# All SBUF tiles begin at one place in a line of 256 bytes, and the small vectors get a pool of their own

## The chip, the core and the metric

The kernel runs on one core of a Trainium2 chip. The core has a matrix engine (TensorE, PE in the profile; its weight loads are listed as PEld), a vector engine (VectorE, DVE), an activation engine (ScalarE, ACT), GpSimd (POOL) and SyncE (SP), whose queue issues nearly all DMAs. Data lies in SBUF, 128 partitions wide; a tile takes the same byte range in every partition. Matmul results go to PSUM. The metric is the device time of one execution in microseconds, as the median of several runs.

## What is computed

One layer of a diffusion backbone over 1024 latent tokens and 256 context tokens, width 1024, all in fp32. In a much shortened form:

```
h       = rms_norm(x) * (1 + m1) + m0                  # m = silu(c) @ w_mod + b_mod
aq, ak, av, bq, bk, bv, cq, cf, cb, ci, cg, gates = split(h @ w_in)
ya      = window_attn(aq, ak, av, context, sink)       # 8 heads, window 128, keys of the context, sink
yb      = global_attn(bq, bk, bv, context)             # 8 heads, 256 + 1024 keys
yc      = hgrn2_bidir(cq, cf, cb, ci, cg, ...)         # 4 heads, recurrence in both directions
x_mix   = x + m2 * ((sum over n of sigmoid(gates_n) * (y_n @ w_branch_n)) @ w_out)
h2      = rms_norm(x_mix) * (1 + m4) + m3
a, g    = split(dwconv(h2 @ w_up))                     # depthwise, 3 taps
out     = rms_norm(x_mix + m5 * ((a * silu(g)) @ w_down))
```

## The kernel before

Every large product is done in three passes: each fp32 operand is split into a high part (a cast to fp32r, on ScalarE) and a low part (the difference, a subtraction on VectorE), and the products high x high, high x low and low x high are summed in PSUM. In `gemm_cm` these are lines L160 (`wh`, `hh`), L161 (`wh`, `hl`) and L162 (`wl`, `hh`), in this order for each of the 128-row blocks of the contraction. The weights are the stationary operand, the activations are the moving one, 512 columns at a time. In `gemm_tm` (L170 to L172) it is the other way round: the moving operand is the weights, 256 columns.

`w_unit` brings a unit of weights: a DMA on SP's queue into `wr` (L142), the cast to `wh` on ScalarE (L145), the difference `wl` on VectorE (L146), three buffers each. The units are requested some steps ahead of the product that reads them.

The stages, with the tiles that stream through TensorE as the moving operand:

- context and latent norm, context projections (`czf`, `czb`, `czv`: moving `chh`, `chl`, 256 columns)
- HGRN2, four heads: projections `zq`, `zf`, `zb`, `zv`, `zg` (moving `hh`, `hl`, 512 columns) and many small matmuls
- token-major projections `tm`, with the products for the gates, `gz` (moving `hh`, `hl`), in between
- window attention and then global attention, 16 iterations each (8 token tiles x 2 groups). Scores of the next iteration, values of the present one and more `gz` products are woven into each other. `values` transposes probabilities (`pp`, L983), splits them (`ph` on ScalarE, L987; `pl` on VectorE, L988) and streams `ph` and `pl` against the values (`po`, L977 and L978). The global scores stream the keys (`sbl`, L1097 and L1098)
- merge (`br`: moving `yh`, `yl`)
- output projection `wo` in two halves of 512 tokens (moving `h2h`, `h2l`, which hold the merged branches there); VectorE adds the residual `xr` (L601), which a DMA on SP's queue brings (L600)
- FFN: `up` (moving `h2h`, `h2l`, now the normed activations) and `dn` (moving `ah`, `al`), in seven groups; the last group (`dl`) and the final norm run in three pieces of 512, 256 and 256 tokens

`softmax_window` and `softmax_global` keep their statistics in small tiles with two buffers each: negated maxima (`wm`, `ng`), sums (`ws`, `sm`), the sink's term (`wk`), factors (`fa`, `mn`). The first instruction that writes a buffer again waits for the last reader of two iterations before; the last one is the scaling of the probabilities on GpSimd (L1070, L1117 and L1119).

The tiles come from pools that lie on two stacks, one from the low end of SBUF, one from the high end (`side="right"`). A tile's place follows from the sizes of what was allocated before it, rounded to 32 bytes. Small tiles (16 bytes, 32 bytes) between large ones shift all that come after them within a line of 256 bytes.

The order in which each engine takes its instructions is fixed when the program is built; priorities (`tc.high_priority`) move the weights' steps ahead.

Of the kernel before, what the change touches and what calls it, by code (L numbers as in the profile page):

```python
# [9 lines left out]
F32 = mybir.dt.float32  # L10
F32R = mybir.dt.float32r
U32 = mybir.dt.uint32
AF = mybir.ActivationFunctionType
# [5 lines left out]
P = 128  # L19
D = 1024  # L20
KT = D // P
# [45 lines left out]
U_C = {"q": 0, "f": 4, "b": 8, "v": 12, "g": 16, "gate": 20}  # L67


class Ctx:  # L70
    pass


def build(tc, ins, out, dbg=None):
    nc = tc.nc
    V, A, G, T, SP = nc.vector, nc.scalar, nc.gpsimd, nc.tensor, nc.sync
    with ExitStack() as top:
        const = top.enter_context(tc.tile_pool(name="const", bufs=1))
        wp = top.enter_context(tc.tile_pool(name="wp", bufs=3))
        ps = top.enter_context(tc.tile_pool(name="ps", bufs=2, space=PSUM))  # L80
        dp = top.enter_context(tc.tile_pool(name="dp", bufs=1, space=DRAM))

        def ct(shape, name, dt=F32):
            return const.tile(shape, dt, tag=name, name=name)

        def dt_(shape, name, dt=F32):
            return dp.tile(shape, dt, tag=name, name=name)
# [5 lines left out]
            return ps.tile(list(shape), dt, tag=tag, name=name)  # L93


        ones = ct([P, P], "ones")
        V.memset(ones, 1.0)
        mhalf = ct([P, 8], "mhalf")
        V.memset(mhalf, -0.5)
        cc = ct([P, KT, 2], "cc")  # L100
        SP.dma_start(cc, ins["cc"])

        tmpv = ct([P, KT, 2], "tmpv")
        A.activation(tmpv, ones[:, :KT * 2].rearrange("p (k v) -> p k v", v=2), AF.Sigmoid)
        A.activation(tmpv, cc, AF.Sigmoid)
        scc = ct([P, KT, 2], "scc")
        V.tensor_tensor(out=scc, in0=cc, in1=tmpv, op=ALU.mult)
        gains = ct([P, 3, KT], "gains")
        SP.dma_start(gains, ins["gains"])
        bmod = ct([P, 48], "bmod")  # L110
        SP.dma_start(bmod, ins["b_mod"])
        ident = ct([P, P], "ident")
        SP.dma_start(ident, ins["ident"])
        lbr = ct([P, 8], "lbr")
        gnc = ct([P, 1], "gnc")
        identr = ct([P, P], "identr", F32R)
        G.tensor_copy(identr, ident)
        mods = ct([P, 4, KT], "mods")
        af = ct([P, KT], "a_ffn")
        m01 = ct([P, KT, 2, 2], "m01")  # L120
        a01 = ct([P, KT, 2], "a01")
        lb = ct([P, 8], "lbt")
        oml = ct([P, 8], "oml")


        q_d = [dt_([LT, P, 512], f"q_d{b}") for b in range(2)]
# [89 lines left out]
            V.scalar_tensor_tensor(out=ohl, in0=t, scalar=bi, in1=ohh.bitcast(F32), op0=ALU.add, op1=ALU.subtract)  # L216

        with ExitStack() as s0:
            xp = s0.enter_context(tc.tile_pool(name="xp", bufs=1, side="right", reuse_waits="tile"))
# [3 lines left out]
            xq = xin.enter_context(tc.tile_pool(name="xq", bufs=1, side="right", reuse_waits="tile"))  # L223
# [3 lines left out]
            xm_ = xw.enter_context(tc.tile_pool(name="xm_", bufs=1))  # L227

            hc = (chh, chl)
            units0 = []  # L230
# [30 lines left out]
            for i in range(KT):  # L261
                wm = xm_.tile([P, 2, KT, P], F32, tag="wm", name=f"wm{i}", bufs=WM)
# [39 lines left out]
            SP.dma_start(lbr, ins["lb"])  # L302
            SP.dma_start(gnc, ins["gn"])

            lt = ct([P, 8], "lt")
# [9 lines left out]
            hp = hpool.enter_context(tc.tile_pool(name="hp", bufs=1, reuse_waits="tile"))  # L315
# [3 lines left out]
            sp_ = stx.enter_context(tc.tile_pool(name="sp_", bufs=1, reuse_waits="tile"))  # L319
# [28 lines left out]
            cp = s0.enter_context(tc.tile_pool(name="cp", bufs=1, reuse_waits="tile"))  # L348
# [52 lines left out]

            weave((ctx_all(), 14), (lat_norm(), 13))
            xin.close()
            cp2 = s0.enter_context(tc.tile_pool(name="cp2", bufs=1, reuse_waits="tile"))

            Fp = cF
            B = 1
# [73 lines left out]


        with ExitStack() as sc:
            c1 = sc.enter_context(tc.tile_pool(name="c1", bufs=1, side="right", reuse_waits="tile"))
# [10 lines left out]


        with ExitStack() as sp3:
            p3 = sp3.enter_context(tc.tile_pool(name="p3", bufs=2, side="right", reuse_waits="tile"))
# [55 lines left out]
        n0 = 10 + GATES_A  # L554
        for br, units in ((0, gates[10:n0]), (1, gates[n0:])):
            with ExitStack() as sa:
                ap_ = sa.enter_context(tc.tile_pool(name=f"at{br}", bufs=2, side="right", reuse_waits="tile"))
# [8 lines left out]
        fp = top.enter_context(tc.tile_pool(name="fp", bufs=1, side="right", reuse_waits="tile"))  # L566
        xm = fp.tile([P, KT, L], F32, tag="xm", name="xm")
        f2 = top.enter_context(tc.tile_pool(name="f2", bufs=1, side="right", reuse_waits="tile"))
        h2h = f2.tile([P, KT, L], F32R, tag="h2h", name="h2h")
        h2l = f2.tile([P, KT, L], F32R, tag="h2l", name="h2l")  # L570
        with ExitStack() as sm:
            mp = sm.enter_context(tc.tile_pool(name="mp", bufs=2, reuse_waits="tile"))
            merge_up(nc, mp, ins, gate_d, y_d, xm, h2h, h2l, w_unit, gemm_cm, mm2)
        f3 = ExitStack()
        ff = f3.enter_context(tc.tile_pool(name="ff", bufs=2, reuse_waits="tile"))
        cw = ff.tile([P, 2 * FT, 4], F32, tag="cw", name="cw", bufs=1)
        SP.dma_start(cw, ins["conv"])

# [13 lines left out]
        for hf in range(2):  # L592
            cols = slice(hf * 512, hf * 512 + 512)
            ss = []
            for i in range(KT):
                w = w_unit(ins["w_out"][i], KT, P)
                z = bank("b", f"wo{hf}{i}", (P, 512))
                gemm_cm(z, w, (h2h, h2l), cols)
                xr = ff.tile([P, 512], F32, tag="o", name=f"xr{hf}{i}", bufs=3)
                SP.dma_start(xr, ins["xT"][i * P:(i + 1) * P, cols])  # L600
                V.scalar_tensor_tensor(out=xm[:, i, cols], in0=z, scalar=mods[:, 0, i:i + 1], in1=xr,  # L601
                                       op0=ALU.mult, op1=ALU.add)
# [43 lines left out]
        for g, ng in enumerate(FFN_GROUPS):  # L646
# [15 lines left out]
            else:  # L662
# [21 lines left out]
                for bi, n in enumerate(LAST):  # L684
# [349 lines left out]
def softmax_window(nc, tl, mm2, tt, g, nm, QT, KH, KL, trir, identr, snk, nsnk, res):  # L1034
    V, A, G, T = nc.vector, nc.scalar, nc.gpsimd, nc.tensor
# [3 lines left out]
    w = nk - 256  # L1039
    m0 = (lo - (tt - 1)) * P  # L1040
    Ps = []
    ng = tl([P, 4], "wm", nm)
    sm = tl([P, 4], "ws", nm)
    sk = tl([P, 4], "wk", nm)
    for h in range(4):

        sc = mm2(f"sa{nm}{h}").rearrange("p a b -> p (a b)")[:, 256:256 + nk]
        T.matmul(sc[:, :256], QT[:, h], KH[:, g, :256], start=True, stop=False)
        T.matmul(sc[:, :256], QT[:, h], KL[:, g, :256], start=False, stop=True)
        k = (2 + lo) * P  # L1050
# [192 lines left out]
```

## Time and profile before

| | us |
|---|---|
| median of 3 runs | 2242.84 |
| lowest and highest run | 2238.89, 2244.82 |
| profiled execution, its own time | 2242.07 |
| span of the profiled execution | 2240.3 |

The granted clock of TensorE over the span is 0.992 of full speed. A profile is one execution. Each row of a group says line, engine, operation, tiles out<-in (moving operand first for a matmul, then the stationary one), shape, count, then busy us and the mean ns of one, then the idle time of the engine just before them and what ended it. Rows of windows say from:to in us of the span, then busy us and the number of records per engine. Rows of the timeline say start, duration, engine, line, operation. A DMA is listed at its issue on SP's queue and by its time to landing.

### The profile page before, as it was taken

Reading aid. Unit: us, or ns where it says so; the run is one execution under the profiler, and the core shown is the slowest. Engines: PE = TensorE matmul, PEld = TensorE weight load, DVE = VectorE, ACT = ScalarE, POOL = GpSimd, SP = SyncE. Lnnn points to the kernel's source line nnn. Section 1 sums busy time; section 2 is a strip of 40 time slices with the busy share of each in tenths; the row PEclk is TensorE's granted clock in tenths of the full one; section 3 lists DMA queues with packets and bytes.
Section 4 is the critical chain, followed back from the end, with each engine's and each line's share of the span. In section 5 each row is a group of like instructions: output and inputs, shape, how many; then the busy total and the mean of one; then the engine's idle time right before and its main releaser. Section 6 shows DMA issues by size and latency. Waiting matters only on the chain. (4 is left out here: it accounts for less than half of the span.)

```text
span 2240.3 us, 30805 instructions
## 1 busy us (share of the span) xinstructions
PE 2158.9 (96%) x11912; PEld 1778.5 (79%) x11912; DVE 1358.5 (61%) x2426; ACT 888.6 (40%) x1618; POOL 285.4 (13%) x297
## 2 busy tenths in 40 slices
PE   7799999999999999999999999999999999999997
PEld 4778887888988888777777788778888888888876
DVE  6946656636665777599998657554434344444345
ACT  4523323311123777677777534332222122222223
POOL 1410011010021222133323100100000000000004
PEclk9999999999999999999999999999999999999999
DMA  8320111126543211301100554421110202111112
GB/s 312 118 65 29 48 48 34 53 93 214 186 150 126 60 46 53 97 21 31 34 29 27 179 178 142 132 85 34 43 61 24 70 21 69 33 56 56 33 52 76
DMA packets 80242, 180.14 MB, mean 80 GB/s; under 512 B 9056, under 2 KB 38240, under 8 KB 79072
## 3 DMA queue, kind: packets, MB, share of 16 engines
q1 hardware_dynamic: 79808, 178.11, 24.5%
q8 instruction: 94, 1.54, 0.3%
q14 instruction: 52, 0.43, 0.1%
q10 hardware_dynamic: 288, 0.07, 0.0%
HBM read 148.26 MB, written 29.88 MB: 80 GB/s over the span
## 5 line engine op out<-in xcount | busy, mean ns | idle before, releaser
L145 ACT CAST wh<-wr 128x1024 fp32r<-128x1024 f32 (+2 forms) x194 | 179.6, 927 | 737.7 <-PE up L161 301.8
L146 DVE TENSOR_TENSOR wl<-wr,wh 128x1024 fp32r<-128x1024 f32 (+2 forms) x189 | 206.8, 1094 | 380.8 <-ACT wh L145 379.0
L161 PE MATMUL up<-h2l,wh 128*128 128x512 f32 x704 | 279.1, 397 | 0.0
L160 PE MATMUL up<-h2h,wh 128*128 128x512 f32 x704 | 278.4, 396 | 0.0
L162 PE MATMUL up<-h2h,wl 128*128 128x512 f32 x704 | 276.5, 393 | 0.0
L988 DVE TENSOR_TENSOR pl<-pp,ph 128x512 fp32r<-128x512 f32 x236 | 158.8, 683 | 9.7 <-ACT ph L987 8.2
L160 PEld LDWEIGHTS up<-h2h,wh 128*128 128x128 f32 x704 | 132.1, 188 | 32.9
L160 PE MATMUL gz<-hh,wh 128*128 128x512 f32 x384 | 155.4, 405 | 2.9 <-ACT gs L450 2.8
L162 PEld LDWEIGHTS up<-h2h,wl 128*128 128x128 f32 x704 | 132.2, 188 | 32.3
L161 PEld LDWEIGHTS up<-h2l,wh 128*128 128x128 f32 x704 | 132.2, 188 | 31.0 <-DVE h2l L216 0.3
L987 ACT CAST ph<-pp 128x512 fp32r<-128x512 f32 x236 | 136.3, 585 | 43.1 <-PE pp L983 40.4
L162 PE MATMUL gz<-hh,wl 128*128 128x512 f32 x384 | 151.5, 395 | 0.0
L161 PE MATMUL gz<-hl,wh 128*128 128x512 f32 x384 | 151.4, 394 | 0.0
L160 PE MATMUL dn<-ah,wh 128*128 128x512 f32 x320 | 125.8, 393 | 0.4
L161 PE MATMUL dn<-al,wh 128*128 128x512 f32 x320 | 125.7, 393 | 0.0
L162 PE MATMUL dn<-ah,wl 128*128 128x512 f32 x320 | 124.7, 390 | 0.0
L660 DVE SCALAR_TENSOR_TENSOR xm<-dn,mods,xm 128x1024 f32<-128x1024 f32 x48 | 61.6, 1283 | 88.7 <-PE dn L162 88.2
L171 PE MATMUL tm<-wl,hh 128*128 128x256 f32 x384 | 108.9, 283 | 2.6 <-DVE wl L146 2.6
L170 PE MATMUL tm<-wh,hh 128*128 128x256 f32 x384 | 108.7, 283 | 0.0
L172 PE MATMUL tm<-wh,hl 128*128 128x256 f32 x384 | 108.6, 283 | 0.0
L977 PE MATMUL po<-ph,VHL 128*128 128x512 f32 x236 | 105.4, 447 | 1.3 <-ACT ph L987 1.3
L978 PE MATMUL po<-pl,VHL 128*128 128x512 f32 x236 | 99.2, 420 | 7.6 <-DVE pl L988 7.3
(825 smaller groups left out, 5045.0 us busy)
## 6 DMA issues: line engine op xcount, KB each, us to landing
wr<-in_w_cm SPq DMA_DIRECT2D x56, 512.0 KB, 3.8
wr<-in_w_up SPq DMA_DIRECT2D x44, 512.0 KB, 3.6
wmr<-in_w_mod SPq DMA_DIRECT2D x32, 512.0 KB, 4.6
gate_d<-gs SPq DMA_DIRECT2D x48, 256.0 KB, 2.3
sgt<-gate_d SPq DMA_DIRECT2D x24, 512.0 KB, 3.8
wm<-in_w_mod SPq DMA_DIRECT2D x8, 1024.0 KB, 14.2
wr<-in_w_tm SPq DMA_DIRECT2D x16, 512.0 KB, 3.8
wr<-in_w_out SPq DMA_DIRECT2D x16, 512.0 KB, 3.8
```

Of the source, the lines that this page charges most:

```text
L145: A.copy(hi[:, :n], raw[:, :n])
L146: (lo_eng or V).tensor_tensor(out=lo[:, :n], in0=raw[:, :n], in1=hi[:, :n].bitcast(F32), op=ALU.subtract)
L160: T.matmul(psl, wh[:, k, c], hh[:, k0 + k, cols], start=s, stop=False)
L161: T.matmul(psl, wh[:, k, c], hl[:, k0 + k, cols], start=False, stop=False)
L162: T.matmul(psl, wl[:, k, c], hh[:, k0 + k, cols], start=False, stop=e)
L170: T.matmul(psl, hh[:, k, toks], wh[:, k % 4, :], start=s, stop=False)
L171: T.matmul(psl, hh[:, k, toks], wl[:, k % 4, :], start=False, stop=False)
L172: T.matmul(psl, hl[:, k, toks], wh[:, k % 4, :], start=False, stop=e)
L977: T.matmul(po, vv, ph, start=n == 0, stop=False)
L978: T.matmul(po, vv, pl, start=False, stop=n == len(kts) - 1)
L987: A.copy(ph, pp)
L988: V.tensor_tensor(out=pl, in0=pp, in1=ph.bitcast(F32), op=ALU.subtract)
```

## The change

1. A class `Aligned` wraps every SBUF pool. It rounds a tile's free size up to a multiple of 64 fp32 numbers, 256 bytes, and returns a view of the part that was asked for.
2. The vectors of a few numbers (`ones`, `mhalf`, `cc`, `scc`, `gains`, `bmod`, `mods`, `lbr` and others) go to a pool `small`, which isn't wrapped; a tile `rest` fills it up. `ones` shrinks from 128 columns to the 16 that are read. `lb`, `oml` and `lt` become slices of one tile.
3. A tile `edge` of 96 bytes at the top of the right stack brings that stack to the same place in the line as the left one.
4. `xr` has two buffers and not three.
5. The statistics of the softmaxes become slices of one tile `st` (two buffers).

Where tiles begin, in bytes within a line of 256, by the addresses of the two built programs:

| tiles | before | after |
|---|---|---|
| wr, wh, wl; wm; hh, hl; cK, cF, cV; yh, yl, y, sgt | 128 | 128 |
| chh, chl | 224 | 128 |
| cx, x32, their squares | 192 | 128 |
| HGRN2: qr, KS, QQ, Vt, S, KC; ST, kt, yo, ys | 224; 160 | 128 |
| tables and outputs of the token-major stage; wmr | 160 | 128 |
| KH, KL, VHL; pw, plat, pc, ph, pl, yT | 224 | 128 |
| QT, qf, qs (window; global) | 32; 224 | 128 |
| xm, h2h, h2l | 224 | 128 |
| xr, squares of the output projection | 64 | 128 |
| u, sg, ah, al, ht | 192 | 128 |

The low-end stack as a whole moves down by one line of 256 bytes: hh began at 220 x 256 + 128, now at 219 x 256 + 128; hl, wr, wh, wl, yh and yl likewise. h2h and h2l keep their line (511 and 639) and move within it.

```diff
+class Aligned:
+    def __init__(self, pool):
+        self.pool = pool
+    def tile(self, shape, dt, **kw):
+        n = math.prod(shape[1:])
+        m = -(-n // 64) * 64
+        if m == n:
+            return self.pool.tile(shape, dt, **kw)
+        t = self.pool.tile([shape[0], m], dt, **kw)[:, :n]
...
-        const = top.enter_context(tc.tile_pool(name="const", bufs=1))
-        wp = top.enter_context(tc.tile_pool(name="wp", bufs=3))
+        const = Aligned(top.enter_context(tc.tile_pool(name="const", bufs=1)))
+        small = top.enter_context(tc.tile_pool(name="small", bufs=1))
+        small.tile([P, 48], F32, tag="rest", name="rest")
+        wp = Aligned(top.enter_context(tc.tile_pool(name="wp", bufs=3)))
...
+        edge = top.enter_context(tc.tile_pool(name="edge", bufs=1, side="right"))
+        edge.tile([P, 24], F32, tag="edge", name="edge")
...
-        f2 = top.enter_context(tc.tile_pool(name="f2", bufs=1, side="right", reuse_waits="tile"))
+        f2 = Aligned(top.enter_context(tc.tile_pool(name="f2", bufs=1, side="right", reuse_waits="tile")))
...
-                xr = ff.tile([P, 512], F32, tag="o", name=f"xr{hf}{i}", bufs=3)
+                xr = ff.tile([P, 512], F32, tag="o", name=f"xr{hf}{i}", bufs=2)
...
-    ng = tl([P, 4], "wm", nm)
-    sm = tl([P, 4], "ws", nm)
-    sk = tl([P, 4], "wk", nm)
+    st = tl([P, 8, 4], "st", nm)
+    ng, sm, sk = st[:, 0], st[:, 1], st[:, 2]
...
-    ng = tl([P, 2, 4], "ng", nm)
-    sm = tl([P, 2, 4], "sm", nm)
-    mn = tl([P, 4], "mn", nm)
-    fa = tl([P, 2, 4], "fa", nm)
+    st = tl([P, 8, 4], "st", nm)
+    ng, sm, fa, mn = st[:, 0:2], st[:, 2:4], st[:, 4:6], st[:, 6]
```

Every engine's instructions keep their order, with one exception on SP's queue in the output projection. `xr02` is the residual block of the third output tile of the first half, `wr91` the weights of the seventh; what an instruction waits for stands in brackets. Before:

```order
L600 DMA xr01_13976<-in_xT 128x512 [waits DMAHW3_49,PE_49]
L600 DMA xr02_14013<-in_xT 128x512 [waits DMAHW4_49]
L600 DMA xr03_14050<-in_xT 128x512 [waits DMAHW5_49,DMAHW2_49,DVE_49]
L142 DMA wr91_14129<-in_w_out 128x1024 [waits DMAHW6_49,DVE_49]
L600 DMA xr04_14087<-in_xT 128x512 [waits DMAHW7_49,DMAHW3_49,DVE_49]
L142 DMA wr92_14166<-in_w_out 128x1024 [waits DMAHW0_49,DVE_49]
```

And now:

```order
L623 DMA xr01_13902<-in_xT 128x512 [waits DMAHW3_49,PE_49]
L623 DMA xr02_13939<-in_xT 128x512 [waits DMAHW4_49,DMAHW2_49,DVE_49]
L166 DMA wr91_14055<-in_w_out 128x1024 [waits DMAHW5_49,DVE_49]
L623 DMA xr03_13976<-in_xT 128x512 [waits DMAHW6_49,DMAHW3_49,DVE_49]
L166 DMA wr92_14092<-in_w_out 128x1024 [waits DMAHW7_49,DVE_49]
```

The residual's DMA that waits for the first product on VectorE is now the third and not the fourth, and each later one stands one place further back relative to the weights; the weights keep their order and their own wait on VectorE.

On VectorE the order stays, and one wait moves. The third iteration of the window attention (`sa` are its scores), before:

```order
L1056 TENSOR_REDUCE wm_2__6768<-sa_0_6771 128x1 [waits PE_49]
L988 TENSOR_TENSOR pl_10_6793<-pp_6787,ph_10_6792 128x512 [waits Activation_49]
L1058 TENSOR_TENSOR wm_2__6768<-wm_2__6768,nsnk_0_6284 128x1 [waits DVE_49]
L1056 TENSOR_REDUCE wm_2__6768<-sa_1_6799 128x1 [waits PE_49]
L1065 TENSOR_TENSOR wk_2__6770<-snk_0_6282,wm_2__6768 128x1 [waits DVE_49]
L953 SCALAR_TENSOR_TENSOR qs_q_7063<-qf_q_7061,qs_q_7063 128x4x64 [waits DMAHW3_49]
L1067 TENSOR_TENSOR ws_2__6769<-ws_2__6769,wk_2__6770 128x1 [waits Activation_49,Pool_49]
```

And now:

```order
L1078 TENSOR_REDUCE st_2__6770<-sa_0_6771 128x1 [waits PE_49,Pool_49]
L1011 TENSOR_TENSOR pl_10_6793<-pp_6787,ph_10_6792 128x512 [waits Activation_49]
L1080 TENSOR_TENSOR st_2__6770<-st_2__6770,nsnk_0_6290 128x1 [waits DVE_49]
L1078 TENSOR_REDUCE st_2__6770<-sa_1_6799 128x1 [waits PE_49]
L1087 TENSOR_TENSOR st_2__6770<-snk_0_6288,st_2__6770 128x1 [waits DVE_49]
L976 SCALAR_TENSOR_TENSOR qs_q_7061<-qf_q_7059,qs_q_7061 128x4x64 [waits DMAHW3_49]
L1089 TENSOR_TENSOR st_2__6770<-st_2__6770 128x1 [waits Activation_49]
```

The wait for GpSimd (`Pool`) moved from the first sum to the first maximum, six instructions ahead; it is for the same GpSimd instruction, the last scaling of two iterations before. In the global attention the like wait moved from the exponentials on ScalarE to the maximum on VectorE ahead of them.

More of the change, by code (lines that the diff above doesn't have):

```diff
@@ L67 @@
 U_C = {"q": 0, "f": 4, "b": 8, "v": 12, "g": 16, "gate": 20}
-class Ctx:
-    pass
+class Aligned:
[7 more added lines that the diff above has]
+        t = self.pool.tile([shape[0], m], dt, **kw)[:, :n]
+        if len(shape) == 2:
+            return t
+        d = "abc"[:len(shape) - 1]
+        return t.rearrange(f"p ({' '.join(d)}) -> p {' '.join(d)}", **dict(zip(d, shape[1:])))
 def build(tc, ins, out, dbg=None):
@@ L77, in build, with cs @@
     with ExitStack() as top:
[L78 to L79 removed]
+        const = Aligned(top.enter_context(tc.tile_pool(name="const", bufs=1)))
+        small = top.enter_context(tc.tile_pool(name="small", bufs=1))
+        small.tile([P, 48], F32, tag="rest", name="rest")
+        wp = Aligned(top.enter_context(tc.tile_pool(name="wp", bufs=3)))
         ps = top.enter_context(tc.tile_pool(name="ps", bufs=2, space=PSUM))
         dp = top.enter_context(tc.tile_pool(name="dp", bufs=1, space=DRAM))
+        edge = top.enter_context(tc.tile_pool(name="edge", bufs=1, side="right"))
+        edge.tile([P, 24], F32, tag="edge", name="edge")
         def ct(shape, name, dt=F32):
             return const.tile(shape, dt, tag=name, name=name)
+        def cs(shape, name, dt=F32):
+            return small.tile(shape, dt, tag=name, name=name)
         def dt_(shape, name, dt=F32):
@@ L113, in build @@
         SP.dma_start(ident, ins["ident"])
-        lbr = ct([P, 8], "lbr")
-        gnc = ct([P, 1], "gnc")
+        lbr = cs([P, 8], "lbr")
+        gnc = cs([P, 1], "gnc")
         identr = ct([P, P], "identr", F32R)
         G.tensor_copy(identr, ident)
[L118 to L123, printed above, removed]
+        mods = cs([P, 4, KT], "mods")
+        af = cs([P, KT], "a_ffn")
+        m01 = cs([P, KT, 2, 2], "m01")
+        a01 = cs([P, KT, 2], "a01")
+        lbs = cs([P, 3, 8], "lbs")
+        lb, oml, lt = lbs[:, 0], lbs[:, 1], lbs[:, 2]
         q_d = [dt_([LT, P, 512], f"q_d{b}") for b in range(2)]
@@ L218, in build @@
         with ExitStack() as s0:
-            xp = s0.enter_context(tc.tile_pool(name="xp", bufs=1, side="right", reuse_waits="tile"))
+            xp = Aligned(s0.enter_context(tc.tile_pool(name="xp", bufs=1, side="right", reuse_waits="tile")))
             chh = xp.tile([P, KT, LC], F32R, tag="chh", name="chh")
@@ L222, in build @@
             xin = s0.enter_context(ExitStack())
-            xq = xin.enter_context(tc.tile_pool(name="xq", bufs=1, side="right", reuse_waits="tile"))
+            xq = Aligned(xin.enter_context(tc.tile_pool(name="xq", bufs=1, side="right", reuse_waits="tile")))
             cx = xq.tile([P, KT, LC], F32, tag="cx", name="cx")
@@ L314, in build @@
             hpool = top.enter_context(ExitStack())
-            hp = hpool.enter_context(tc.tile_pool(name="hp", bufs=1, reuse_waits="tile"))
+            hp = Aligned(hpool.enter_context(tc.tile_pool(name="hp", bufs=1, reuse_waits="tile")))
             hh = hp.tile([P, KT, L], F32R, tag="hh", name="hh")
@@ L403, in build @@
             xin.close()
-            cp2 = s0.enter_context(tc.tile_pool(name="cp2", bufs=1, reuse_waits="tile"))
+            cp2 = Aligned(s0.enter_context(tc.tile_pool(name="cp2", bufs=1, reuse_waits="tile")))
             Fp = cF
@@ L483, in build @@
         with ExitStack() as sc:
-            c1 = sc.enter_context(tc.tile_pool(name="c1", bufs=1, side="right", reuse_waits="tile"))
+            c1 = Aligned(sc.enter_context(tc.tile_pool(name="c1", bufs=1, side="right", reuse_waits="tile")))
             masks = c1.tile([P, NMASK, HB], U32, tag="masks", name="masks")
@@ L497, in build @@
         with ExitStack() as sp3:
-            p3 = sp3.enter_context(tc.tile_pool(name="p3", bufs=2, side="right", reuse_waits="tile"))
+            p3 = Aligned(sp3.enter_context(tc.tile_pool(name="p3", bufs=2, side="right", reuse_waits="tile")))
             cs = p3.tile([P, LT, 2, 32], F32, tag="cs", name="cs", bufs=1)
@@ L556, in build @@
             with ExitStack() as sa:
-                ap_ = sa.enter_context(tc.tile_pool(name=f"at{br}", bufs=2, side="right", reuse_waits="tile"))
+                ap_ = Aligned(sa.enter_context(tc.tile_pool(name=f"at{br}", bufs=2, side="right", reuse_waits="tile")))
                 nf = 16 * len(units)
@@ L563, in build @@
         hpool.close()
-        fp = top.enter_context(tc.tile_pool(name="fp", bufs=1, side="right", reuse_waits="tile"))
+        fp = Aligned(top.enter_context(tc.tile_pool(name="fp", bufs=1, side="right", reuse_waits="tile")))
         xm = fp.tile([P, KT, L], F32, tag="xm", name="xm")
-        f2 = top.enter_context(tc.tile_pool(name="f2", bufs=1, side="right", reuse_waits="tile"))
+        f2 = Aligned(top.enter_context(tc.tile_pool(name="f2", bufs=1, side="right", reuse_waits="tile")))
         h2h = f2.tile([P, KT, L], F32R, tag="h2h", name="h2h")
```

27 lines of the change are left out of this document (13 added, 14 removed).

## The prediction

> **What bounds the kernel now.** I read the page's first two parts, then the busy time by stage, then the start times of single matmuls.
>
> ```profile
> span 2240.3 us, 30805 instructions
> PE 2158.9 (96%) x11912; PEld 1778.5 (79%) x11912; DVE 1358.5 (61%) x2426; ACT 888.6 (40%) x1618; POOL 285.4 (13%) x297
> PE   7799999999999999999999999999999999999997
> ```
>
> TensorE is busy from the second slice to the last but one. Busy time by stage (window and its length, then busy us and number of records for PE, PEld, DVE, ACT, POOL; the granted clock, the DMA share and GB/s):
>
> ```profile
> 723.00:936.00 213.00, 210.38 (x1240) 178.65 (x1239) 155.99 (x469) 152.90 (x385) 49.52 (x64) 1.00 0.21 65
> 936.00:1246.00 310.00, 289.94 (x1621) 231.26 (x1620) 280.02 (x667) 232.37 (x552) 102.07 (x128) 1.00 0.11 35
> 1246.00:1386.60 140.60, 139.08 (x619) 112.92 (x618) 85.47 (x79) 59.77 (x64) 0.00 (x0) 1.00 0.54 174
> 1386.60:1480.00 93.40, 92.57 (x405) 73.82 (x405) 50.15 (x62) 32.47 (x41) 10.59 (x7) 1.00 0.42 136
> 1480.00:2180.00 700.00, 699.15 (x3016) 564.06 (x3015) 304.56 (x283) 168.27 (x184) 1.02 (x1) 1.00 0.15 46
> ```
>
> The rows are window attention, global attention, merge, output projection and FFN. In the FFN the PE works 699 of 700 us at full clock, VectorE 305, ScalarE 168, the DMAs 15%. So there the time is matmuls times the distance from one start to the next, and nothing else comes near. In the global attention VectorE (280 of 310) is nearly as full as the PE (290).
>
> A matmul's record (390 ns) overlaps its neighbour's, so I take starts, not durations. First and last L160 of four stretches in the order of time, and the number of records in the same stretches:
>
> ```profile
> 159.03 0.39 PE L160 MATMUL zv<-hh,wh 128*128 128x512 f32 x1
> ...
> 169.24 0.39 PE L160 MATMUL zv<-hh,wh 128*128 128x512 f32 x1
> ...
> 1400.04 0.40 PE L160 MATMUL wo<-h2h,wh 128*128 128x512 f32 x1
> ...
> 1420.34 0.40 PE L160 MATMUL wo<-h2h,wh 128*128 128x512 f32 x1
> ...
> 1600.10 0.39 PE L160 MATMUL dn<-ah,wh 128*128 128x512 f32 x1
> ...
> 1620.01 0.39 PE L160 MATMUL dn<-ah,wh 128*128 128x512 f32 x1
> ...
> 1700.15 0.39 PE L160 MATMUL up<-h2h,wh 128*128 128x512 f32 x1
> ...
> 1719.75 0.39 PE L160 MATMUL up<-h2h,wh 128*128 128x512 f32 x1
> ```
>
> ```profile
> 158.80:169.67 10.87, 10.87 (x49) 1.00 0.14 49
> 1400.04:1421.03 20.99, 20.99 (x91) 1.00 0.46 152
> 1600.10:1620.68 20.58, 20.58 (x91) 1.00 0.22 64
> 1700.15:1721.14 20.99, 20.99 (x91) 1.00 0.10 25
> ```
>
> The lines follow each other in threes (L160, L161, L162), so the pairs lie 45, 87, 87 and 84 matmuls apart. Start to start: zv 10.21/45 = 226.9 ns, wo 20.30/87 = 233.3, dn 19.91/87 = 228.9, up 19.60/84 = 233.3. (Each count holds one record that began before the window.) Four streams of the same shape, with the same kind of weights, no waits and clock 1.00, run at three speeds. What goes along with the speed is where the moving operand begins in a 256-byte line (table of the section on the change): hh at 128, ah and al at 192, h2h and h2l at 224. The weights begin at 128 in all four.
>
> **The change, part by part.** Groups that carry the sum (busy us, mean ns of one record, idle before):
>
> ```profile
> L160 PE MATMUL up<-h2h,wh 128*128 128x512 f32 x704 | 278.4, 396 | 0.0
> L160 PE MATMUL gz<-hh,wh 128*128 128x512 f32 x384 | 155.4, 405 | 2.9 <-ACT gs L450 2.8
> L160 PE MATMUL dn<-ah,wh 128*128 128x512 f32 x320 | 125.8, 393 | 0.4
> L160 PE MATMUL br<-yh,wh 128*128 128x512 f32 x192 | 74.4, 390 | 1.1 <-DVE xm L1156 1.1
> L160 PE MATMUL wo<-h2h,wh 128*128 128x512 f32 x128 | 51.1, 401 | 0.3 <-ACT h2h L1161 0.3
> L160 PE MATMUL zv<-hh,wh 128*128 128x512 f32 x64 | 24.9, 389 | 0.0
> L977 PE MATMUL po<-ph,VHL 128*128 128x512 f32 x236 | 105.4, 447 | 1.3 <-ACT ph L987 1.3
> L1097 PE MATMUL sbl<-KH,QT 128*128 128x512 f32 x128 | 51.8, 404 | 0.0
> ```
>
> *New starts.* The three lines of each projection have the same count, L977/L978 and L1097/L1098 too. After the change every moving operand begins at 128, as hh does now, so I give all of them zv's 226.9 ns.
> - up: 3 x 704 = 2112 matmuls x (233.3 - 226.9 = 6.4 ns) = 13.5 us.
> - wo: 3 x 128 = 384 x 6.4 = 2.5 us.
> - dn: 3 x 320 = 960 x 2.0 = 1.9 us; the 512-column part of the last group (dl, 8 tiles x 6 = 48 matmuls, as the code has it) 0.1 us.
>
> These 18.0 us lie on the path in full, since the PE there waits for nothing. Their other end: yh, also at 128, has a mean record of 390 ns against zv's 389; 1 ns on 3504 matmuls is 3.5 us less.
> - Attention: 256 sbl and 472 po move from 224 to 128: at most 728 x 6.4 = 4.7 us. VectorE is nearly as busy there and the PE has gaps, so the gain lies between 0 and 4.7; I take the middle, 2.3.
> - gz streams hh, which begins at 128 before and after: nothing. But its mean record (405) is above zv's (389) where it stands among other matmuls; its three lines average some 9 ns over zv, 1152 x 9 = 10 us with waits in it. If half comes from neighbours at 224, another 5 us go. I take 0 and keep 5 for the low end.
>
> Shorter matmuls I count at nothing: 256 columns that begin at 128 (tm) and at 224 (czv) have the same mean record:
>
> ```profile
> L171 PE MATMUL tm<-wl,hh 128*128 128x256 f32 x384 | 108.9, 283 | 2.6 <-DVE wl L146 2.6
> L161 PE MATMUL czv<-chl,wh 128*128 128x256 f32 x32 | 9.1, 284 | 0.2 <-DVE chl L216 0.2
> L1141 DVE TENSOR_TENSOR yl<-y,yh 128x1024 fp32r<-128x1024 f32 x12 | 14.7, 1224 | 9.2 <-ACT yh L1140 8.9
> L636 DVE TENSOR_TENSOR al<-u,ah 128x1024 fp32r<-128x1024 f32 x22 | 26.9, 1224 | 20.0 <-ACT ah L635 20.0
> L1162 DVE TENSOR_TENSOR h2l<-xm,h2h 128x1024 fp32r<-128x1024 f32 x8 | 9.8, 1226 | 10.9 <-ACT h2h L1161 10.9
> ```
>
> The last three rows say that VectorE doesn't mind: the same subtraction on tiles at 128, 192 and 224 takes 1224 to 1226 ns. The weights' DMAs land at 128 before and after: 0.
>
> *xr with two buffers.* Its DMA now waits for the product two steps back, not three; the weights behind it on SP's queue keep the wait that they have.
>
> ```profile
> 1395.16 0.75 DVE L601 SCALAR_TENSOR_TENSOR xm<-wo,mods,xr 128x512 f32<-128x512 f32 x1 [1.72 <-DMA xr<-in_xT]
> 1404.44 0.75 DVE L601 SCALAR_TENSOR_TENSOR xm<-wo,mods,xr 128x512 f32<-128x512 f32 x1 [3.48 <-PE wo L162]
> DMA to landing us min/median/max: 2.5/2.6/4.5
> ```
>
> xr02 can go out when the first product ends (1395.9) and lands at the latest 4.5 us later, 1400.4; its reader starts at 1404.4. That is 4 us of slack: cost 0. With twice the longest landing it would be late by 0.5 us; in all 14 steps and passed on to the PE, 7 us.
>
> *One statistics tile in attention.* The wait for GpSimd two iterations back moves ahead to the first maximum (windows), and from ScalarE to VectorE (global). Behind it on VectorE stand the pl subtractions that release the PE.
>
> ```profile
> L1070 POOL TENSOR_SCALAR pw<-pw,ws__6502 x4: 693/696/701, 731.6 to 737.3; 128x512 f32<-128x512 f32 x4
> L1056 DVE TENSOR_REDUCE wm__6768<-sa x4: 814/821/824, 746.3 to 752.2; 128x1 f32<-128x640 f32 x4
> ```
>
> GpSimd's last scaling for iteration 0 starts at 737.3 and takes 0.7 us; the maximum of iteration 2 starts at 746.3, 8 us later: 0. The shorter memset of ones and the small vectors' new place touch nothing on the path.
>
> *Sum.* 18.0 + 2.3 = 20.3 us, against the profiled execution's 2242.07 us (span 2240.3): 2221.8, say **2222 us**. The runs shown have a median of 2242.84 and lie between 2238.89 and 2244.82, so the profiled execution is a usual one.
>
> **Rivals.**
> *The start has no part in it.* The speeds could belong to something else that distinguishes the stages. For it: dn alternates between values, so the distance isn't a plain constant for each tile. Against: wo and up differ in stage, in DMA load (152 and 25 GB/s) and in output, and share only h2h and h2l; both have 233.3. Time 2242. The Trainium skill speaks for this rival: its page "SBUF — State Buffer", section "Specifications (TRN2)", gives lines of 16 bytes, and all starts of before are multiples of 32, so by it nothing is to be won; no run here shows such a line. Its page "TensorE: Matmul & The Clock Gate", section "Back-to-back issue gap", has a gap made of the columns alone (estimate for 512: 215.8 ns, no term for an address); the trace's three speeds disagree.
>
> *The line is 512 bytes.* All fast tiles of before (hh, hl, yh, yl) begin in an even 256-byte line, at 128 of 512; the slow ones (ah at 448, h2h at 480) in odd lines. The change shifts the left stack by one line, so hh, hl, yh, yl and the weights come to 384 of 512. If that were a slow place, 1152 gz, 960 z and 576 br matmuls would pay up to 6.4 ns, 17.2 us, and h2h, also at 384, would gain nothing: 2259 us. It decides from the point where 384 is as bad as 480. Against it: speed falls with the bytes left in the line (64 left 228.9, 32 left 233.3), and 384 leaves 128.
>
> *More than the forecast*: all of the attention's and gz's bounds on the path: 2242.1 - 18.0 - 4.7 - 5 = 2214.
>
> **How the numbers follow.** Forecast, with the larger gain as its low end: 0.88, own range 2214 (just above) to 2228 (no attention gain, 3.5 us off up, wo and dn). No effect: 0.07. Slower by the wider line: 0.05. The runs of before scatter by 3 us to either side, so the range is 2211 to 2231; what lies outside is the two rivals and a little of the forecast. What this kernel's measurement can tell from no change is about 0.3%, 6.7 us: faster 0.88, same 0.07, slower 0.05.
>
> **What would show it.** Start to start in up and wo falls from 233.3 to 226.9, in dn from 228.9; mean records of up fall from 396 to about 389; zv and br stay. The FFN's window shrinks by some 15 us with PE still full. The forecast is wrong if up keeps 233, if zv or br grow, or if the PE in the FFN gets gaps. A product L601 that waits for xr, or a maximum L1056 that waits for GpSimd, would mend the terms that I put at 0.

## The result and the profile after

| | before | after |
|---|---|---|
| median of 4 runs each, us | 2241.97 | 2224.50 |
| lowest and highest run | 2238.89, 2244.82 | 2222.04, 2227.34 |
| profiled execution, its own time | 2242.07 | 2222.04 |
| span of the profiled execution | 2240.3 | 2220.3 |

The ratio after to before is 0.9923, 95% interval 0.9905 to 0.9941: faster by 17.5 us, where 20.3 were forecast. The profiled execution happens to be the fastest of the four.

The head of the page of the changed kernel, and how full TensorE is in each of 40 slices:

```profile
span 2220.3 us, 30792 instructions
PE 2136.9 (96%) x11912; PEld 1777.1 (80%) x11912; DVE 1358.7 (61%) x2426; ACT 888.2 (40%) x1618; POOL 283.3 (13%) x297
PE   7789999999999999999999999999999999999997
```

TensorE has the same 11912 matmuls and 22.0 us less of busy time; it is still what bounds the kernel. Where that time went shows in the busy time by stage, each window going from about the stage's first matmul to the next stage's. From the top: window attention, global attention, output projection, FFN. Before:

```profile
712.30:936.10 223.80, 221.18 (x1305) 187.27 (x1303) 161.99 (x483) 162.50 (x408) 49.52 (x64) 1.00 0.22 67
936.10:1246.20 310.10, 290.04 (x1621) 231.38 (x1619) 280.19 (x668) 232.44 (x552) 102.07 (x128) 1.00 0.11 35
1386.60:1480.30 93.70, 92.87 (x407) 74.12 (x407) 50.45 (x62) 32.77 (x41) 10.59 (x7) 1.00 0.42 136
1480.30:2196.60 716.30, 715.38 (x3084) 577.01 (x3083) 316.32 (x294) 174.22 (x190) 1.02 (x1) 1.00 0.15 45
```

After:

```profile
710.30:935.10 224.80, 220.59 (x1303) 187.61 (x1303) 161.88 (x483) 162.30 (x408) 49.49 (x64) 1.00 0.22 67
935.10:1244.30 309.20, 289.31 (x1621) 231.76 (x1620) 279.92 (x668) 232.51 (x552) 101.79 (x128) 1.00 0.11 35
1384.20:1476.00 91.80, 90.43 (x407) 74.12 (x406) 50.50 (x62) 32.80 (x42) 10.74 (x7) 1.00 0.43 139
1476.00:2176.60 700.60, 699.35 (x3084) 576.88 (x3083) 316.46 (x294) 174.35 (x190) 1.02 (x1) 1.00 0.15 46
```

The FFN is 15.7 us shorter and the output projection 1.9 us; window attention is 1.0 us longer and global attention 0.9 us shorter, together nothing. 15.7 + 1.9 = 17.6 us, which is the 17.5 us of the medians. The two profiled executions lie 20.0 us apart; of the rest, 1.9 us are the earlier start of the merge, which differs by more than that between kernels with the same distances up to there (shown below), and 0.5 us are the merge itself, 139.9 us after 140.4.

The groups of the changed kernel that answer to those of the prediction (busy us, mean ns of one):

```profile
L184 PE MATMUL up<-h2h,wh 128*128 128x512 f32 x704 | 273.8, 389 | 0.0
L184 PE MATMUL gz<-hh,wh 128*128 128x512 f32 x384 | 155.7, 406 | 2.3 <-ACT gs L473 2.2
L184 PE MATMUL dn<-ah,wh 128*128 128x512 f32 x320 | 124.9, 390 | 0.7
L184 PE MATMUL wo<-h2h,wh 128*128 128x512 f32 x128 | 50.0, 392 | 0.8 <-ACT h2h L1181 0.8
L1000 PE MATMUL po<-ph,VHL 128*128 128x512 f32 x236 | 104.8, 444 | 1.3 <-ACT ph L1010 1.3
L1117 PE MATMUL sbl<-KH,QT 128*128 128x512 f32 x128 | 51.5, 403 | 0.0
```

up fell from 396 to 389 and wo from 401 to 392; gz, po and sbl (405, 447 and 404 before) hardly moved.

Start to start is the sharper measure. A window that begins at the start of one matmul and ends at the start of another, with nothing but large matmuls between, has a known number of them in it: 48 for zv, 176 for wo, 384 for up, 192 for dn. (The count in the row is one or two higher, since neighbours' records reach in.) Columns: from:to, length, busy us and records of TensorE, clock, DMA share, GB/s. Before, in the order zv, wo, up, dn:

```profile
158.80:169.68 10.88, 10.88 (x49) 1.00 0.14 49
1438.47:1479.54 41.07, 41.07 (x178) 1.00 0.38 122
1638.32:1727.92 89.60, 89.60 (x385) 1.00 0.11 33
1594.36:1638.32 43.96, 43.96 (x193) 1.00 0.25 77
```

After:

```profile
157.56:168.44 10.88, 10.88 (x49) 1.00 0.15 49
1435.31:1475.25 39.94, 39.94 (x178) 1.00 0.42 132
1630.58:1717.62 87.04, 87.04 (x385) 1.00 0.12 35
1717.62:1761.14 43.52, 43.52 (x193) 1.00 0.24 78
```

Divided: zv 226.7 before and after, wo 233.4 to 226.9, up 233.3 to 226.7, dn 229.0 to 226.7 ns. Every step predicted for these four products came.

Two waits could have taken some of it back. In the changed kernel, what VectorE waited for ahead of the residual's product L624, and ahead of the window maxima L1078 (us, times):

```profile
  PE wo L186: 34.7, 12
  DMA xr<-in_xT: 1.8, 1
```

```profile
  PE sa L1075: 11.1, 16
  PE pp L1006: 2.1, 2
```

The residual's DMA is waited for once, 1.8 us (before, once too, 1.72 us; the wait of 3.48 us in the prediction's second row is for TensorE). The window maxima never wait for GpSimd, and by the same view of L1108 and L1120 the global maxima don't either.

### The profile page after: what moved, and what is told of

Same layout as the page of the kernel before. It is cut to its first block, busy times and chain, and to the rows that moved or that the text cites. A ratio compares the mean times of both kernels' runs of the same rounds, so it can differ in the third digit from the quotient of the medians.

```text
span 2220.3 us, 30792 instructions
## 1 busy us (share of the span) xinstructions
PE 2136.9 (96%) x11912; PEld 1777.1 (80%) x11912; DVE 1358.7 (61%) x2426; ACT 888.2 (40%) x1618; POOL 283.3 (13%) x297
## 5 line engine op out<-in xcount | busy, mean ns | idle before, releaser
L185 PE MATMUL up<-h2l,wh 128*128 128x512 f32 x704 | 273.9, 389 | 0.0
L184 PE MATMUL up<-h2h,wh 128*128 128x512 f32 x704 | 273.8, 389 | 0.0
```

The costliest lines, as they stand in the source:

```text
L184: T.matmul(psl, wh[:, k, c], hh[:, k0 + k, cols], start=s, stop=False)
L185: T.matmul(psl, wh[:, k, c], hl[:, k0 + k, cols], start=False, stop=False)
```

## The experiments

The prediction says that the speed goes along with where the moving operand itself begins in a line of 256 bytes. A rival fits the same rows: what counts is how far the moving operand begins from the weights that are loaded beside it. Before, the weights lay at 128 everywhere, so the two could not be told apart. Each edit below is to the changed kernel unless it says otherwise. Places are by the addresses of the built programs. "d" is the start of the moving operand less that of the weights, within 256 bytes.

**Only the right stack back.** The tile at the top of the right stack goes, so h2h and h2l begin at 224 again; the left stack stays at 128.

```diff
-        edge.tile([P, 24], F32, tag="edge", name="edge")
+        pass
```

> The change without the 96-byte tile at the top of the right stack: the right stack (h2h, h2l, KH, KL, ph, pl, HGRN2 tiles) begins at 224 again, the left one (weights, hh, yh, ah) stays at 128. Theory (the start of the moving operand in the 256-byte line sets the distance between matmuls): wo and up go back to 233.3 ns, dn, zv, br stay at 226.7; 2496 x 6.6 = 16.5 us more than the change, about 2241, all of it in the output projection and the FFN's up products, and next to nothing in the attention. Rival (the gain comes from the left stack, from small vectors or from ah): wo and up stay at 226.7, time 2225.

2241.59 us, ratio to before 0.9997 (0.9989 to 1.0006). up and dn:

```profile
1640.04:1729.65 89.61, 89.61 (x385) 1.00 0.11 33
1596.49:1640.04 43.55, 43.55 (x193) 1.00 0.26 78
```

up is back at 233.4 ns (89.61/384), dn (ah now at 128) stays at 226.8. The 2 us of dn are too small for the total to show. So the gain hangs on the place of the right stack, and up shows that in it h2h and h2l count.

**The left stack moved instead.** `rest` grows by 96 bytes: weights, hh, hl, yh, yl, ah and al begin at 224, h2h and h2l stay at 128.

```diff
-        small.tile([P, 48], F32, tag="rest", name="rest")
+        small.tile([P, 72], F32, tag="rest", name="rest")
```

> The change with the left stack moved on by 96 bytes: weights, hh, hl, yh, yl, ah, al begin at 224, the right stack (h2h, h2l) stays at 128. Theory (the moving operand's own start): up and wo keep 226.7 though their weights now begin at 224; zv, br and dn go to 233.3, together 2496 matmuls outside attention and gz x 6.6 = 16.5 us, and some of 1152 gz, so 2241 to 2248. Rival 1 (the distance between the starts of moving operand and weights): zv, br, dn keep 226.7, up and wo, now 96 bytes off, slow to about 233; 2241. Rival 2 (the weights' start): all slow to 233.3, 2257 or more.

2242.35 us, ratio 1.0002 (0.9994 to 1.0011): the whole gain is gone. zv, up, dn:

```profile
159.41:170.29 10.88, 10.88 (x49) 1.00 0.15 49
1637.66:1727.63 89.97, 89.97 (x386) 1.00 0.11 33
1594.14:1637.66 43.52, 43.52 (x193) 1.00 0.25 78
```

This run decides. hh and ah begin at 224, the place that I had called slow, and stream at 226.7 ns; h2h begins at 128, the place that I had called fast, and streams at 234.3. My theory falls. What the fast streams share is d = 0. The total alone would not have told, since my theory had expected 2241 to 2248 us here and the rule of the distance 2241.

**Everything at 0.** Both stacks are filled up so that every large tile begins at 0 of 256.

```diff
-        small.tile([P, 48], F32, tag="rest", name="rest")
+        small.tile([P, 80], F32, tag="rest", name="rest")
-        edge.tile([P, 24], F32, tag="edge", name="edge")
+        edge.tile([P, 56], F32, tag="edge", name="edge")
```

> The change with both stacks moved so that all large tiles begin at 0 of the line. Theory as a number of bytes left in the first line (32 left 233.3 ns, 64 left 228.9, 128 left 226.7): 256 left is at least as good, 226.7 or up to 1 ns less; 2220 to 2225. Rival (a fixed cost of 13 ns per matmul over 512 columns at 2.4 per ns comes from the broken first line): 213 to 220 ns, 3500 to 6000 matmuls x 7 to 13 ns, 2150 to 2200. Rival (0 is a place like 224): 233, 2240 or more.

2222.81 us, ratio 0.9916 (0.9902 to 0.9929), whose interval overlaps that of the change. up:

```profile
1635.66:1722.70 87.04, 87.04 (x385) 1.00 0.11 34
```

The same 226.7 ns as at 128: the place itself is worth nothing, the common place is.

**The kernel before with the edge alone.** No `Aligned`, no pool for small vectors, no merged statistics; only the 96 bytes at the top of the right stack, and two buffers for xr.

```diff
+        edge = top.enter_context(tc.tile_pool(name="edge", bufs=1, side="right"))
+        edge.tile([P, 24], F32, tag="edge", name="edge")
...
-                xr = ff.tile([P, 512], F32, tag="o", name=f"xr{hf}{i}", bufs=3)
+                xr = ff.tile([P, 512], F32, tag="o", name=f"xr{hf}{i}", bufs=2)
```

> The kernel before with two edits only: the 96-byte tile at the top of the right stack, and xr with two buffers (the room that the tile needs). h2h, h2l and most of the right stack begin at 128, ah and al stay at 192, the small tiles stay where they were. Theory: wo and up at 226.7, dn at 228.9 as before: 2242 - 16.5 = 2225.5, within 2 to 3 us of the whole change. Rival (the small vectors' pool or the softmax tiles carry the gain): 2242.

2227.38 us, ratio 0.9934 (0.9922 to 0.9947). up and dn:

```profile
1633.49:1720.58 87.09, 87.09 (x385) 1.00 0.12 34
1589.52:1633.49 43.97, 43.97 (x193) 1.00 0.25 77
```

up has 226.8 ns; dn, whose ah is still at 192, keeps 229.0. The kernel before had a median of 2241.73 us beside it, so this one tile carries 14.4 us of the change's 17.5. Of the rest, dn's 960 x 2.3 = 2.2 us are accounted for; the remaining 0.9 us are less than the intervals tell apart.

**The side effects alone.** The kernel before with two buffers for xr and the statistics in one tile per iteration, with nothing aligned. (The new tile shifts the window attention's keys and values from 224 to 160 and its QT from 32 to 224; h2h, h2l, ah and al stay where they were.)

```diff
-                xr = ff.tile([P, 512], F32, tag="o", name=f"xr{hf}{i}", bufs=3)
+                xr = ff.tile([P, 512], F32, tag="o", name=f"xr{hf}{i}", bufs=2)
-    ng = tl([P, 4], "wm", nm)
...
+    st = tl([P, 8, 4], "st", nm)
+    ng, sm, sk = st[:, 0], st[:, 1], st[:, 2]
```

> The kernel before with two of the change's side effects and no alignment: two buffers for xr instead of three, and the statistics vectors of the softmaxes in one tile each. The right stack stays where it was apart from those vectors. Prediction's steps (both cost nothing): 2242 us, ratio to before 1.000 within 0.002, up at 233.3 ns and dn at 229 ns. Rival (they cost or gain something that the alignment hid or paid for): a ratio off by more than 0.002 either way.

2243.03 us, ratio 1.0001 (0.9992 to 1.0009): they cost nothing and bring nothing that the total shows.

**Other distances.** The right stack alone moves, by the size of `edge`; the weights stay at 128.

```diff
-        edge.tile([P, 24], F32, tag="edge", name="edge")
+        edge.tile([P, 56], F32, tag="edge", name="edge")
```

That puts h2h at 0; 40 numbers put it at 64, 16 at 160, and 8 at 192.

> The change with the right stack at 0 and the left one at 128: up and wo have their moving operand 128 bytes from their weights in the line of 256. Theory (the distance between moving operand and weights, period 256): not 226.7; with the values so far (64: 228.9, 96: 233.3, 160: 234.3) some 234 or more, 2241 or more. If the period is 128: 226.7. Old theory (the moving operand's own start): 226.7, as with everything at 0. zv, br and dn keep 226.7 in every theory.

> The change with the right stack at 64: distance -64 (192) in up and wo. Theory of the distance, if it counts alike to both sides: about 229, 6 us over the change; if it grows with the distance one way: 234 or more. Old theory (own start, 192 bytes left): 226.7. zv, br, dn 226.7.

> The change with the right stack at 160: distance 32. Theory of the distance: between 226.7 and 228.9, 2 to 4 us over the change. Old theory (own start, 96 bytes left): 227 to 228. It tells the shape of the curve near 0. zv, br, dn 226.7.

> The changed kernel with the right stack at 192 instead of 128: the moving h2h begins 64 bytes after the weights in its line, the distance that only dn of the kernel before had (228.9 ns there). If the value belongs to the distance: wo and up at 229 ns, some 2112 x 2.2 + 384 x 2.2 = 5.5 us more than the changed kernel, about 2230 us. If 228.9 belonged to dn's own tiles: up at 233.3 ns as at all other distances, about 2240 us.

One run each: 2237.90, 2240.39, 2236.92 and 2230.95 us. The first three lie up to 3.5 us apart at one pace of up, so I go by the starts. The 384 matmuls of up, one fence for each kernel in this order:

```profile
1636.53:1726.12 89.59, 89.59 (x385) 1.00 0.12 34
```

```profile
1638.03:1727.63 89.60, 89.60 (x386) 1.00 0.11 33
```

```profile
1634.65:1724.26 89.61, 89.61 (x385) 1.00 0.12 33
```

```profile
1635.64:1723.55 87.91, 87.91 (x385) 1.00 0.11 34
```

With the runs above, for 512 columns:

| d in bytes | ns, start to start | seen in |
|---|---|---|
| 0 | 226.7 | zv, up and dn of the changed kernel; up, everything at 0; dn and zv at 224 |
| 32 | 233.4 | up, h2h at 160 |
| 64 | 229.0, 228.9 | dn before; up, h2h at 192 |
| 96 | 233.3 | up before |
| 128 | 233.3 | up, h2h at 0 |
| 160 | 234.3 | up, left stack at 224 |
| 192 | 233.3 | up, h2h at 64 |

It isn't a matter of how far apart: 32 bytes cost as much as 96, and 64 bytes, alone, a third of it. The run at 192 answers whether 228.9 belonged to dn's own tiles: it belongs to the distance. The run at 160 had been expected between 226.7 and 228.9 ns and misses that. d = 224 was not tried.

At d = 0 the 226.7 ns hold for unbroken streams. At the start of the changed kernel's FFN a few small matmuls stand among those of up. The first row is 10 matmuls of up soon after them, the second 35 of up, 2 us further on:

```profile
1481.70:1484.02 2.32, 2.32 (x12) 1.00 0.01 5
1486.21:1494.14 7.93, 7.93 (x36) 1.00 0.01 2
```

That is 232 ns and then 227, with the same tiles, the same clock and hardly any DMA. So a common start isn't the whole of the rule; why the pace takes some matmuls to settle, no run here shows.

**One of the three products off.** The low part of the weights, wl, gets a pool of its own at 224; wh and all moving operands stay at 128. Of each three matmuls two have d = 0 and one has d = 160.

```diff
+        lag = top.enter_context(tc.tile_pool(name="lag", bufs=1))
+        lag.tile([P, 24], F32, tag="lag", name="lag")
+        wpl = top.enter_context(tc.tile_pool(name="wpl", bufs=3))
+        lag2 = top.enter_context(tc.tile_pool(name="lag2", bufs=1))
+        lag2.tile([P, 40], F32, tag="lag2", name="lag2")
...
-                lo = wp.tile([P, 1024], F32R, tag="wl", name=f"wl{cnt[0]}", bufs=WL)
+                lo = wpl.tile([P, 1024], F32R, tag="wl", name=f"wl{cnt[0]}", bufs=WL)
```

> The change with the low weights wl alone moved to 224; wh and all moving operands stay at 128. One matmul in three, L186 (wl), has its own weights at a distance of 160 from the moving operand. If the distance to its own weights counts, the three intervals sum to 680 + 7.6 = 687.6 ns and the longer one is that which L186 starts; if the distance to the weights that are loaded meanwhile counts (those of the next matmul), the sum is the same and the longer one is that which L185 starts, the one before. If one bad neighbour spoils all, 3 x 234.3 = 703. About 6144 matmuls of 512 columns x 2.5 ns = 15 us more than the change, 2240, in the first two cases.

One run, 2249.19 us, beside 2243.07 of the kernel before. zv, up and dn:

```profile
158.44:169.60 11.16, 11.16 (x49) 1.00 0.15 48
1644.10:1733.42 89.32, 89.32 (x385) 1.00 0.11 33
1599.45:1644.10 44.65, 44.65 (x193) 1.00 0.25 77
```

All three take 232.5 to 232.6 ns on the average of the three passes, zv and dn too, which had been fast. Neither way of counting that I had set down gives this: with one matmul in three paying the 234.3 - 226.7 = 7.6 ns of d = 160, the average would be 229.2. One odd operand slows the stream nearly as much as if every pair were off. The starts don't single out one pair: in up, the intervals that begin at L189, L190 and L191 (hh x wh, hl x wh, hh x wl) are 233.3, 231.7 and 232.7 ns on average, so none of the three keeps 226.7.

**256 columns.** In the run with the right stack at 64, a stretch of 30 matmuls of czv and czf (256 columns, chh and chl at 64, weights at 128) and one of 41 of czf and czb:

```profile
72.24:75.64 3.40, 3.40 (x32) 1.00 0.00 0
85.75:90.58 4.83, 4.83 (x44) 1.00 0.70 212
```

113.3 and 117.8 ns. The DMA share, 0.00 and 0.70 in these rows, is not what tells them apart. In the same run, 18 czf matmuls and 18 czv matmuls:

```profile
45.30:47.42 2.12, 2.12 (x21) 1.00 0.13 50
81.26:83.30 2.04, 2.04 (x21) 1.00 0.77 241
```

117.8 ns with the DMAs nearly idle, 113.3 with them busy. The same 30 matmuls as in the first fence, in the changed kernel at d = 0, and behind them 184 matmuls of tm:

```profile
72.93:76.53 3.60, 3.60 (x33) 1.00 0.00 0
559.80:581.87 22.07, 22.07 (x185) 1.00 0.41 134
```

120.0 and 119.9 ns. So the common start isn't the best for this shape. tm's 1152 matmuls can be put at the same distance: their weights, here the moving operand, get a pool at 64, with hh and hl left at 128; a control has the same pool at 128.

```diff
+            lag = sp3.enter_context(tc.tile_pool(name="lag", bufs=1, side="right", reuse_waits="tile"))
+            lag.tile([P, 16], F32, tag="lag", name="lag")
+            wt = sp3.enter_context(tc.tile_pool(name="wt", bufs=3, side="right", reuse_waits="tile"))
...
-                    ws = [w_unit(ins["w_tm"][(br * 3 + u) * 2 + kh], 4, 256) for kh in range(2)]
+                    ws = [w_unit(ins["w_tm"][(br * 3 + u) * 2 + kh], 4, 256, pool=wt) for kh in range(2)]
```

The control has 64 numbers in `lag` and not 16.

> The changed kernel, but the weights of the token-major stage (1152 matmuls of 256 columns, the weights are the moving operand, hh and hl the stationary one) lie in a pool of their own on the right stack that begins at 64 instead of 128, so that the moving operand begins 64 bytes before the stationary one in its line. Theory (the interval hangs on the distance between the starts of the two operands, and for 256 columns the best distance is 64 bytes before, as 256-column matmuls of czv, czf and czb showed in the run with the right stack at 64): tm's interval falls from 119.96 to 113.3 ns; the stage gives up to 1152 x 6.6 ns = 7.6 us, so the time falls from 2224.5 to between 2216 and 2221. Rival (what czv showed belongs to its own tiles): tm stays at 119.96 ns and the time at 2224. A loss here would come from the three more weight buffers of each kind or from the first loads of that pool.

> The control of tm64: the same pool of its own for the token-major weights, but beginning at 128 like hh, distance 0. Both theories: tm's interval stays at 119.96 ns as in the changed kernel. What this run differs by from the changed kernel (2224.5 us) is what the second pool and its loads are worth; what tm64 differs by from this run is the distance alone.

2221.21 us, ratio 0.9900 (0.9886 to 0.9913), and for the control 2222.92 us, 0.9910 (0.9896 to 0.9923). 184 matmuls of tm, first at 64, then the control:

```profile
556.65:578.32 21.67, 21.67 (x185) 1.00 0.44 146
```

```profile
560.10:582.17 22.07, 22.07 (x185) 1.00 0.43 143
```

117.8 against 119.9 ns. The distance has an effect on tm too, but a third of what I expected: 1152 x 2.2 = 2.5 us, and the medians' 1.7 us are inside the intervals. No version here beats the changed kernel by more than the measurement can tell.

## Why the prediction was right, and where it was not

*What bounds the kernel.* Right: the time is matmuls times the distance from start to start, and VectorE, ScalarE and DMA time in the FFN stayed as they were.

*"What goes along with the speed is where the moving operand begins in a 256-byte line."* This step failed, though the time came out. It is where the moving operand begins against the weights; the run with the left stack at 224 shows it. The forecast held because the change puts both at 128, where the two rules agree; that they do is luck. The prediction's rows had the weights at 128 throughout, so they could not tell the rules apart. A change that moved every moving operand to 128 and the weights elsewhere would have been forecast faster; in the run with the left stack at 224, h2h stood at 128 and up still took 234.3 ns.

*up, 13.5 us; dn, 1.9; dl, 0.1.* Right in size, and right that fewer ns per matmul go into the time in full; what makes them fewer is the distance and not the start. 15.5 us forecast, 15.7 measured over the FFN. By the long windows up would gain 2112 x 6.7 = 14.1 us and dn 960 x 2.3 = 2.2, 0.6 us more than the stage shows.

*wo, 2.5 us.* TensorE's busy time in that stage fell by 92.87 - 90.43 = 2.4 us; the stage became 1.9 us shorter, since TensorE now stands idle there for 1.4 us and not 0.8.

*Attention, 2.3 us out of 0 to 4.7.* Mis-sized, and the 18.0 us without it were nearer. sbl and po were never off: keys and QT of the global attention, ph, pl and VHL all began at 224 before the change, d = 0, and their records stayed (404 to 403, 447 to 444 ns). With the right rule the table of starts would have given 0 ahead of the run. This term follows from the step that failed. One product of the window attention did come to d = 0, its scores sa (256 and 384 columns; keys at 224 and QT at 32 before), which the prediction counted at nothing. Their records did not get shorter, before and after:

```profile
L1051 PE MATMUL sa<-KH,QT 128*128 128x384 f32 x48 | 16.4, 342 | 0.0
L1073 PE MATMUL sa<-KH,QT 128*128 128x384 f32 x48 | 16.6, 346 | 0.0
```

The earlier start of the merge in the profile of after isn't attention either. The merge's first matmul with the right stack at 224, with the left stack at 224, and with everything at 0:

```profile
1248.96 0.39 PE L184 MATMUL br<-yh,wh 128*128 128x512 f32 x1
```

```profile
1244.88 0.39 PE L184 MATMUL br<-yh,wh 128*128 128x512 f32 x1
```

```profile
1249.56 0.40 PE L184 MATMUL br<-yh,wh 128*128 128x512 f32 x1
```

The first two lie 4 us apart, in kernels of the same total time. The third is 5.1 us later than in the changed kernel (1244.50), with every distance in the attention 0 in both. Its profiled execution took 2226.89 us, and the four others of that kernel 2222.04 to 2223.63, so a start some us earlier or later goes along with the scatter of executions.

*gz, 0 with 5 kept.* Right at 0: hh and the weights had d = 0 before and after, and the record is 405 and 406 ns. What it has over zv's 389 is not a neighbour's place. gz is woven into other products, and where two gz matmuls follow each other directly they stand 229 ns apart on average, before and after, not 226.7; this fits the pace behind a break, shown above, but was not tested.

*Shorter matmuls, 0.* Right for this change, for a reason that doesn't carry: tm was at d = 0 before, and czv at 224 (d = 96) happened to have the same mean record (284 and 283 ns; that is the shortest of czv's three lines, the others have 291 and 297). With the moving operand 64 bytes before the stationary one, 256 columns take 113.3 or 117.8 ns.

*xr, statistics, small vectors, 0.* Right: 1.0001 with the first two alone. The small vectors were not moved alone; the run with only the right stack back has their pool, and comes to the time of before.

*Rivals.* That the start has no part is out. By the rule of the Trainium skill, page "TensorE: Matmul & The Clock Gate", section "Step-by-step: what each phase is for", loading the next weights takes no read bandwidth from the running matmul, since the two have ports of their own. Taken as a rule of speed, that leaves no room for the place of the weights to matter. The runs here show that it does, 226.7 to 234.3 ns with the distance, and the measurement decides. That the line is 512 bytes is out as well: weights, hh and h2h begin at 384 of 512 in the changed kernel and ah at 128 of 512, and all stream at 226.7 ns. The larger gain, 2214, needed attention and gz, which had nothing to give.

## What to carry to other kernels

Where TensorE streams without pause, take its start-to-start time per product from a long window, and compare it between products of one shape; a per cent or three of difference at the same clock is worth a look at the addresses. For products like these, with 512 columns and new weights for each matmul, set the start of the moving operand and that of the weights to the same place modulo 256 bytes; for 256 columns measure first. Here one 96-byte tile did five sixths of it, and a single operand out of step, wl, cost more than the whole gain. Before a property of one operand is named as the cause, check that something else in the same rows isn't constant: one run that moves the other operand would have told.

## What the runs showed of the hardware

- The distance between the starts of moving operand and weights, modulo 256 bytes, sets the pace of unbroken streams of 512-column fp32r matmuls that each load new weights: 226.7 ns at 0, 228.9 at 64, 233.3 to 234.3 at 32, 96, 128, 160 and 192. Behind a break up took 232 ns for some matmuls at distance 0 too. What inside the chip does it, no run here shows.
- One odd tile slows more than its own matmuls: with wl at distance 160 and wh at 0, zv, up and dn took 232.5 to 232.6 ns on average, and none of the three lines of up kept 226.7 (one kernel, one run).
- 256 columns behave otherwise: 119.9 ns at distance 0; with the moving operand 64 bytes before the stationary one, 113.3 ns in some stretches of one kernel and 117.8 in others (czf has both), and 117.8 in tm. It is not the DMA load; what chooses between the two is open.
